# Up-projections of a ConvFFN: low parts of the input sums and of the first pair by adding transfers, and down's first pair prepared within the last pair of chunks

## The chip, the cores and the metric

The kernel runs on one core of a Trainium2 chip, in one launch. The metric is the device time of that launch in microseconds (us), and the time of a kernel is the median of several runs. The kernel before takes 1107.46 us (median of 3 runs, 1106.6 to 1108.25).

## The reference

The kernel computes a trunk of two layers over 512 tokens of 1024 features, in float32. Each layer is an attention mixer (a dilated window in the first, a forgetting attention in the second) and then a gated feed-forward network with a causal convolution of width 3 over the tokens. The change touches the feed-forward network (FFN) alone:

```python
def conv_ffn(xn, w_up, cw, cb, w_down):        # xn (1, 512, 1024), w_up (1024, 5632), w_down (2816, 1024)
    a = xn @ w_up
    T = a.shape[1]
    ap = jnp.pad(a, ((0, 0), (CONV_W - 1, 0), (0, 0)))
    a = sum(ap[:, j:j + T] * cw[j] for j in range(CONV_W)) + cb
    gate, val = jnp.split(a, 2, axis=-1)
    return (jax.nn.gelu(gate, approximate=True) * val) @ w_down
...
    h = h + rms_norm(mix, g[1])
    f = conv_ffn(rms_norm(h, g[2]), w_up[l], conv_w[l], conv_b[l], w_down[l])
    h = h + rms_norm(f, g[3])
```

## The kernel before

**High and low.** Each float32 product of two matrices is made of three matmuls on rounded operands (`mm3`, L294): high by high (L295), high by low (L296) and low by high (L297). So each operand, a weight or an activation, has to be split first: a high part, which is a rounded copy that the scalar engine (ACT) makes, and a low part, the operand less its high part. There are two ways to a low part. Either the vector engine (DVE) subtracts, once the high is there. Or ACT writes the negative of the rounded operand into the low's place ("minus"), and a transfer that GpSimd (POOL) issues adds the operand itself to it. The names are `added` in the pairs (L740 to 742), and `minus` and `low_added` for plain pieces.

**Weights.** A weight piece is 128x1024, 512 KB. The class `Weights` loads pieces by transfers from SyncE's queue, each as soon as a buffer is free, and splits them in the order of use: `high` (L58 the rounded copy, L69 the minus), `low` (L76, on DVE), `low_added` (L96). `ahead` says how many pieces `get` splits beyond the one that it hands out.

**The up-projection.** The 5632 columns are 22 chunks of 128 gate and 128 value columns. Chunks 0 to 3 are plain: one piece for the gate and one for the value, eight steps of `mm3` each. Chunks 4 to 19 are taken in eight pairs (`PAIRS`, two chunks each) by a scheme of seven products in place of eight: the four blocks of a pair's weights (A11, A21, A22 and A12: gate or value, first or second half of the features) are joined to S3 = A11 - A21, S1 = A21 + A22, S2 = S1 - A11 and S4 = A12 - S2, and tensor runs A11, S2, S3, A12, S1, A22 and S4, each of 24 matmuls on 128x256, in this order; A11 of the next pair comes between A22 and S4. The factors on the side of x are parts of x itself or sums of them, XA and XB, which `sums_in` makes once (L695 to L715) while chunks 0 to 3 run. Chunks 20 and 21 are plain again.

**The steps of a pair.** `prepare(p)` is a generator whose eight steps (up to a `yield` each) load, join and split a pair's weights, while tensor runs the pair before it: the high of A11; its low; S3's sum and high; the sum S1 (L756); the sum S2 (L758), its high, the high of A12; the lows of S2 (DVE) and A12 (GpSimd, L738), S1's high and adding transfer; the low of S3, the sum S4 (GpSimd, L770, which overwrites A12's raw tile in place), A22's high and adding transfer; and last S4's high and adding transfer. For the first pair the steps run while the plain chunks 2 and 3 run. In the loop over the pairs, `begin` runs product A11, `keep_first` copies it out of PSUM into `csum` (ACT, L1022), `sums` adds products together (DVE, L1044), and `ends` adds the last two (L1029, L1030). Product S2 writes the other half of the banks that `keep_first` reads, and product A12 adds into the first half again, while `sums` reads S2's half; each waits until those reads are done.

**Behind a chunk** stand the convolution's taps (ACT L670 or L657 scales and adds the bias, DVE L664 adds the two shifted taps), the gelu (ACT L689) and the product of gate and value (GpSimd L686), which a GpSimd transfer stores to DRAM (`hD`, L684).

**The down-projection** takes pairs of chunks by the same scheme: `pair_load` reads the activations back from `hD` (SyncE), `pair_sums` (DVE, L807 to L809) joins them, `pair_highs` (ACT, L817) and `pair_lows` (DVE, L821) split three operands of a pair. The first pairs are prepared while the last plain chunks run.

**The order.** Each engine runs its instructions in the order in which the code writes them; nothing is reordered. An instruction waits for its operands and for its buffers, and all that stands behind it on its engine waits with it. The buffers come from pools (16 tiles of 8 KB per partition, 10 of 4 KB, 8 of 2 KB, 8 PSUM banks), so a tile is free again when its last reader is done.

Of the kernel before, what the change touches and what calls it, by code (L numbers as in the profile page):

```python
# [115 lines left out]
def trunk_kernel(ctx, tc, x, norm_gains, w_qkv_a, w_o_a, w_q_b, w_o_b, kv_norm, w_kvf, b_f,  # L116
# [451 lines left out]
    def first_products(bd, n):  # L568
        bd.norm(3)
        outs = [bank([128, T], name="first") for _ in range(n)]  # L570
        ws = []
        for i, o in enumerate(outs):
            if i == 1:
                W.ahead -= 1
            ws.append(W.get())
            feat_mm(ws[i], bd.xT, o, LO)
            if i < 2:
                bd.transpose(2 + i)
            if i == 1:
                W.ahead += 1  # L580
        for w, o in zip(ws, outs):
            feat_mm(w, bd.xT, o, HI)
        return outs
# [65 lines left out]
    def ffn(l, bd, cp, nxt, ahead):  # L649
# [49 lines left out]
        def sums_in():  # L699
# [11 lines left out]
            for X, src in ((XA, v[0]), (XB, v[1])):  # L711
                X += [t8([128, 4, T], F32R, name="xsh"), t8([128, 4, T], F32R, name="xsl")]
                for k in (0, 2):
                    act.copy(X[0][:, k:k + 2], src[:, k:k + 2])
                    dve.tensor_tensor(X[1][:, k:k + 2], src[:, k:k + 2], X[0][:, k:k + 2].bitcast(F32), ALU.subtract)  # L715
                    yield
# [11 lines left out]
        def prepare(p):  # L728

# [13 lines left out]
            ga = grab(2)  # L745
            high("A11", ga)
            yield
            low("A11", ga)
            yield
            va = grab(1)  # L750
            s3 = t4([128, 1024], name="wsum")
            dve.tensor_tensor(s3, ga, va, ALU.subtract)
            high("S3", s3)
            yield
            vb = grab(1)
            dve.tensor_tensor(va, va, vb, ALU.add)  # L756
            yield
            dve.tensor_tensor(ga, va, ga, ALU.subtract)  # L758
            high("S2", ga)
            gb = grab(1)  # L760
            high("A12", gb)
            yield
            low("S2", ga)
            low("A12", gb, pool)
            high("S1", va)
            added("S1", va)
            W.load(W.n_split + 2)
            yield
            low("S3", s3)
            pool.tensor_tensor(gb, gb, ga, ALU.subtract)  # L770
            high("A22", vb)
# [7 lines left out]
        def prepare_last():  # L779

            W.load(W.n_split + 2)
            yield
            yield
            for added in (False, True, False, False):
                W.high(added)
                (W.low_added if added else W.low)()
                yield


# [188 lines left out]
        extra = sums_in()  # L978
        next(extra)
        post(0, first[0:2])  # L980
        next(extra)
        post(1, first[2:4])
        W.ahead = 1
        W.split(base + 7)
        W.high_added()
        steps = prepare(PAIRS[0])
        before = None
        for c in (2, 3):
            banks = [bank([128, T], name="up") for _ in range(2)]
            for s in range(2):  # L990
# [8 lines left out]
                for _ in range(3):  # L999
                    next(extra, None)  # L1000
                next(steps)
            before = c, banks
# [32 lines left out]
        for p in PAIRS:  # L1035
# [16 lines left out]
            bbs = [biased(*pend[0][:2])]  # L1052
            next(steps)
            times(p, "S3", o3, True)
# [33 lines left out]
        for _ in steps:  # L1088
            pass
        pair_sums(0)  # L1090
        banks = [begun[1], bank([128, T], name="up")]
# [4 lines left out]
        glu(pend[0][0], taps(*pend[0][:2]))  # L1096
        pair_highs(0)
        pair_sums(1)
        up(W.get(), banks[1], range(KD))
        post(*pend[1][:2])  # L1100
        before = NF - 2, banks
        banks = [bank([128, T], name="up") for _ in range(2)]
        up(W.get(), banks[0], range(KD))
        product()
        glu(before[0], taps(*before, lambda: pair_lows(0)))
        pair_highs(1)
        pair_sums(2)
        up(W.get(), banks[1], range(KD))
        before = NF - 1, banks
        post(*before, lambda: pair_lows(1))  # L1110
        pair_highs(2)
# [833 lines left out]
```

## Time and profile before

| | |
|---|---|
| median of 3 runs | 1107.46 us (1106.6 to 1108.25) |
| profiled execution, its time and its span | 1105.87 us, 1104.1 us |
| granted TensorE clock, mean | 0.993 |
| TensorE matmuls (PE), busy | 1083.4 us, 98% |
| TensorE weight loads (PEld) | 960.3 us, 87% |
| VectorE (DVE) | 900.8 us, 82% |
| ScalarE (ACT) | 683.8 us, 62% |
| GpSimd (POOL) | 306.8 us, 28% |
| transfers, mean | 220 GB/s |

The busy shares are means over a span in which stages with different limits follow one another: attention, feed-forward, attention, feed-forward. The places of FFN 1 that the prediction speaks of lie between 196 and 421 us; FFN 2 has the same ones some 583 us later. A row of the timeline gives the start in us, the length in us, the engine, the line, the operation, the tile written and those read, and in brackets how long the engine had been idle before it, and what ended that. A row of the windows gives the stretch, its length and then for each engine (matmul, weight load, DVE, ACT, POOL) the busy time and the count, then the granted clock, the transfers' share and the GB/s.

### The profile page before, as it was taken

How to read it: one execution, taken by the hardware profiler on the slowest of the kernel's cores; microseconds unless marked ns; L12 is line 12 of the kernel's file. 1: busy time of each engine (PE TensorE's matmuls, PEld its weight loads, DVE VectorE, ACT ScalarE, POOL GpSimd, SP SyncE). 2: the span in 40 equal slices, each digit the busy share in tenths (PEclk: the TensorE clock that was granted, in tenths of full speed). 3: DMA queues.
4: the chain of work that ended last, by engine and by line, in shares of the span. 5: the costliest groups of instructions: out<-in, count | busy, mean ns of one | idle time of the engine just before them, and what ended most of it. 6: DMA issues, size and time to landing. Idle time of an engine off the chain costs nothing.

```text
span 1104.1 us, 18905 instructions
## 1 busy us (share of the span) xinstructions
PE 1083.4 (98%) x6897; PEld 960.3 (87%) x6897; DVE 900.8 (82%) x1462; ACT 683.8 (62%) x1133; POOL 306.8 (28%) x318
## 2 busy tenths in 40 slices
PE   9999999979999999999999999999979999999997
PEld 7988889879999988888888888889879999987886
DVE  5898979868888799997686677868858888889995
ACT  6645765557676666576451577755467677656573
POOL 3543000264565532000001212100155566531000
PEclk9999999989999999999999999999989999999999
DMA  9799954378878978893447857774368878978962
GB/s 295 244 373 407 345 121 116 86 172 192 232 192 213 255 234 299 297 335 104 146 141 246 271 169 208 258 212 134 86 153 188 226 199 199 237 246 300 337 249 77
DMA packets 159509, 242.71 MB, mean 220 GB/s; under 512 B 12864, under 2 KB 106424, under 8 KB 159416
## 3 DMA queue, kind: packets, MB, share of 16 engines
q1 hardware_dynamic: 143784, 189.33, 52.2%
q0 software_dynamic: 14944, 52.18, 20.8%
q8 instruction: 54, 0.88, 0.3%
q14 instruction: 39, 0.32, 0.1%
q10 hardware_dynamic: 688, 0.01, 0.0%
HBM read 172.37 MB, written 39.73 MB: 192 GB/s over the span
## 4 chain that ended last, share of the span: by engine, by line
PE 88%; issue 5%; DVE 3%; ACT 2%; DMA 1%; POOL 1%; SPq 0%; DVEq 0%; POOLq 0%; ACTq 0%
PE up L295 9%; PE up L296 9%; PE up L297 9%; PE acc L297 9%; PE acc L295 8%; PE acc L296 8%; PE v_ps L295 2%; PE v_ps L296 2%; PE v_ps L297 2%; PE qk_ps L1396 2%; PE pT_ps L1786 2%; PE o_ps L1801 2%; PE s_ps L1752 2%; DVE w L821 1%; PE first L297 1%
## 5 line engine op out<-in xcount | busy, mean ns | idle before, releaser
L295 PE MATMUL up<-xsh,w 128*128 128x256 f32 x512 | 146.9, 287 | 12.5 <-ACT csum L1022 12.5
L296 PE MATMUL up<-xsl,w 128*128 128x256 f32 x512 | 146.4, 286 | 0.0
L297 PE MATMUL up<-xsh,w 128*128 128x256 f32 x512 | 146.3, 286 | 0.0
L734 ACT CAST w<-wraw 128x1024 fp32r<-128x1024 f32 x96 | 97.2, 1043 | 76.8 <-DVE wraw L758 59.1
L686 POOL TENSOR_TENSOR hc<-bb 128x512 f32<-128x512 f32 x44 | 76.7, 1743 | 226.6 <-ACT bb L689 143.2
L664 DVE SCALAR_TENSOR_TENSOR bb<-up,conv,bb 128x511 f32<-128x511 f32 (+1 forms) x160 | 118.7, 745 | 6.0 <-ACT bb L670 3.2
L297 PE MATMUL acc<-w 128*128 128x512 f32 (+1 forms) x311 | 120.6, 388 | 1.3 <-DVE w L821 1.3
L295 PE MATMUL acc<-w 128*128 128x512 f32 (+1 forms) x311 | 120.6, 388 | 0.0
L295 PEld LDWEIGHTS up<-xsh,w 128*128 128x128 f32 x512 | 100.0, 195 | 12.9 <-ACT csum L1022 12.9
L296 PE MATMUL acc<-w 128*128 128x512 f32 (+1 forms) x267 | 103.3, 387 | 0.0
L296 PEld LDWEIGHTS up<-xsl,w 128*128 128x128 f32 x512 | 100.0, 195 | 0.0
L297 PEld LDWEIGHTS up<-xsh,w 128*128 128x128 f32 x512 | 99.8, 195 | 0.0
L296 PE MATMUL up<-xbl,w 128*128 128x256 f32 (+1 forms) x256 | 79.3, 310 | 0.0
L296 PE MATMUL up<-xcl,w 128*128 128x256 f32 (+1 forms) x256 | 79.3, 310 | 0.0
L295 PE MATMUL up<-xbh,w 128*128 128x256 f32 (+1 forms) x256 | 79.3, 310 | 0.0
L295 PE MATMUL up<-xch,w 128*128 128x256 f32 (+1 forms) x256 | 79.2, 310 | 0.0
L297 PE MATMUL up<-xch,w 128*128 128x256 f32 (+1 forms) x256 | 79.2, 310 | 0.0
L297 PE MATMUL up<-xbh,w 128*128 128x256 f32 (+1 forms) x256 | 79.2, 309 | 0.0
L76 DVE TENSOR_TENSOR w<-wraw,w 128x1024 fp32r<-128x1024 f32 x54 | 64.5, 1218 | 16.1 <-ACT w L58 15.8
L58 ACT CAST w<-wraw 128x1024 fp32r<-128x1024 f32 x61 | 62.3, 1057 | 17.5 <-PE v_ps L296 6.9
L297 PEld LDWEIGHTS acc<-w 128*128 128x128 f32 x311 | 58.4, 188 | 14.0 <-DVE w L821 2.2
L295 PEld LDWEIGHTS acc<-w 128*128 128x128 f32 x311 | 58.4, 188 | 11.9
(309 smaller groups left out, 3153.6 us busy)
## 6 DMA issues: line engine op xcount, KB each, us to landing
wraw<-in_w_up_dram SPq DMA_DIRECT2D x88, 512.0 KB
w<-wraw POOLq DMA_DIRECT2D x56, 512.0 KB, 5.2
dT<-dsums SPq DMA_DIRECT2D x28, 512.0 KB
dsums<-in_w_down_dram SPq DMA_DIRECT2D x22, 512.0 KB
dsums<-in_w_down_dram SPq DMA_DIRECT2D x44, 256.0 KB
hD<-hc POOLq DMA_DIRECT2D x44, 256.0 KB, 6.2
dact<-hD SPq DMA_DIRECT2D x44, 256.0 KB
wraw<-dT SPq DMA_DIRECT2D x22, 512.0 KB
```

The lines of the kernel that those rows point to most:

```text
L58: (copy or self.nc.scalar.copy)(pair[:, 0], raw)
L76: self.nc.vector.tensor_tensor(pair[:, 1], raw, pair[:, 0].bitcast(F32), ALU.subtract)
L295: pe.matmul(o, ah, bh, start=first, stop=False, skip_group_check=shared)
L296: pe.matmul(o, ah, bl, start=False, stop=False, skip_group_check=shared)
L297: pe.matmul(o, al, bh, start=False, stop=last, skip_group_check=shared)
L664: dve.scalar_tensor_tensor(bb[:, s, n:], ps[:, :T - n], cp[:, 2 - n, ch:ch + 1], bb[:, s, n:], ALU.mult, ALU.add)
L686: pool.tensor_tensor(hc[c], bb[:, 0, :], bb[:, 1, :], ALU.mult)
L734: act.copy(w[a][:, 0], raw)
L1396: pe.matmul(qk_banks[b], a[n == 2], w[n == 1][:, kc % 2, :], start=kc + n == 0, stop=(kc, n) == (KD - 1, 2))
L1752: pe.matmul(sc[j, i][hh][:, :nn], qT[j][own, qp, i * 128:(i + 1) * 128], k[own, kp, :nn], start=qp + kp == 0, stop=qp == 1)
L1786: pe.transpose(o[:, k0 + k, :], p[:, hh, k * 128:(k + 1) * 128], ident)
L1801: pe.matmul(o[64 * hh:64 * hh + 64, i * 128:(i + 1) * 128], Vt[hd // 8][:, k, (hd % 8) * 64:(hd % 8) * 64 + 64], pT[j, i, hh][:, k, :], st ...
```

## The change

There are four parts, in both FFNs. The plain pieces 5 to 7 are split by minus and adding transfer, and `ahead` is set to 2 at the entry. The lows of XA and XB are made by a minus on ACT and an adding transfer in place of a subtraction on DVE. In the first pair of chunks alone, A11, S3 and A12 get their lows by adding transfers too, S2's sum goes to a tile of its own, and the last step (S4's high, minus and transfer) runs after product S2 has been written into the program, not with chunk 3. In the last pair, the four last plain pieces are split two steps earlier, and the steps so gained prepare the first pair of the down-projection; each later `pair_` call stands one place earlier.

```diff
@@ first_products
             if i == 1:
-                W.ahead += 1
+                W.ahead = 2
@@ sums_in
                 for k in (0, 2):
-                    act.copy(X[0][:, k:k + 2], src[:, k:k + 2])
-                    dve.tensor_tensor(X[1][:, k:k + 2], src[:, k:k + 2], X[0][:, k:k + 2].bitcast(F32), ALU.subtract)
+                    s = slice(k, k + 2)
+                    act.copy(X[0][:, s], src[:, s])
+                    act.activation(X[1][:, s], src[:, s], AF.Copy, scale=-1.0)
+                    pool.dma_start(X[1][:, s], src[:, s], accum_op=ALU.add)
                     yield
@@ prepare(p)
+            first = p == PAIRS[0]
...
             high("A11", ga)
+            if first:
+                added("A11", ga)
             yield
-            low("A11", ga)
+            if not first:
+                low("A11", ga)
...
             high("S3", s3)
+            if first:
+                added("S3", s3)
...
-            dve.tensor_tensor(ga, va, ga, ALU.subtract)
-            high("S2", ga)
+            s2 = t4([128, 1024], name="wsum") if first else ga
+            dve.tensor_tensor(s2, va, ga, ALU.subtract)
+            high("S2", s2)
             gb = grab(1)
             high("A12", gb)
+            if first:
+                added("A12", gb)
             yield
-            low("S2", ga)
-            low("A12", gb, pool)
+            low("S2", s2)
+            if not first:
+                low("A12", gb, pool)
...
-            low("S3", s3)
-            pool.tensor_tensor(gb, gb, ga, ALU.subtract)
+            if not first:
+                low("S3", s3)
+            pool.tensor_tensor(gb, gb, s2, ALU.subtract)
@@ prepare_last
-            W.load(W.n_split + 2)
-            yield
-            yield
             for added in (False, True, False, False):
...
+            pair_sums(0)
+            yield
+            pair_highs(0)
+            pair_sums(1)
+            yield
+            pair_lows(0)
+            yield
@@ ffn
         next(extra)
+        for _ in range(2):
+            W.high_added()
         post(0, first[0:2])
         next(extra)
+        W.high_added()
         post(1, first[2:4])
         W.ahead = 1
-        W.split(base + 7)
-        W.high_added()
...
-                next(steps)
+                if (c, s) != (3, 1):
+                    next(steps)
@@ the loop over the pairs
-            next(steps)
+            if p + 1 in PAIRS:
+                next(steps)
             times(p, "S3", o3, True)
@@ behind the pairs
-        pair_sums(0)
...
-        pair_highs(0)
-        pair_sums(1)
+        pair_highs(1)
         up(W.get(), banks[1], range(KD))
         post(*pend[1][:2])
+        pair_sums(2)
...
-        glu(before[0], taps(*before, lambda: pair_lows(0)))
-        pair_highs(1)
-        pair_sums(2)
+        glu(before[0], taps(*before, lambda: pair_lows(1)))
         up(W.get(), banks[1], range(KD))
         before = NF - 1, banks
-        post(*before, lambda: pair_lows(1))
+        post(*before)
```

The next rows are those of ACT in FFN 1 at the end of the first pair's preparation, before the change, from A12's high on (S2's high stands directly ahead of them in both kernels). `w_2314` is A12, `w_2319` S1, `w_2351` A22, `w_2357` S4 and `w_2418` A11 of the next pair; `bb` is a gelu and `csum` the copy of product A11.

```order
L734 CAST w_2314<-wraw_2270 128x1024
L689 ACTIVATE bb_2302<-bb_2302 128x512
L734 CAST w_2319<-wraw_2191 128x1024
L741 ACTIVATE w_2319<-wraw_2191 128x1024
L734 CAST w_2351<-wraw_2223 128x1024
L741 ACTIVATE w_2351<-wraw_2223 128x1024
L734 CAST w_2357<-wraw_2270 128x1024
L741 ACTIVATE w_2357<-wraw_2270 128x1024
L1022 COPY csum_2389<-up_2361 128x256
L1022 COPY csum_2389<-up_2363 128x256
L734 CAST w_2418<-wraw_2312 128x1024
```

The same place of ACT after the change, where the lines are 736 and 743 for 734 and 741, and 1040 for 1022; `w_2324` is A12, `w_2330` S1, `w_2361` A22, `w_2424` S4 and `w_2428` the next A11.

```order
L736 CAST w_2324<-wraw_2279 128x1024
L743 ACTIVATE w_2324<-wraw_2279 128x1024
L689 ACTIVATE bb_2311<-bb_2311 128x512
L736 CAST w_2330<-wraw_2183 128x1024
L743 ACTIVATE w_2330<-wraw_2183 128x1024
L736 CAST w_2361<-wraw_2225 128x1024
L743 ACTIVATE w_2361<-wraw_2225 128x1024
L1040 COPY csum_2395<-up_2367 128x256
L1040 COPY csum_2395<-up_2369 128x256
L736 CAST w_2424<-wraw_2279 128x1024
L743 ACTIVATE w_2424<-wraw_2279 128x1024
L736 CAST w_2428<-wraw_2322 128x1024
```

A12 has a minus more, S4's two operations stand behind the two copies instead of ahead of them, and the next A11 stands behind S4 as it did.

GpSimd's queue at the same place before the change. `hc` is the product of gate and value; `w_2193` is a plain piece, L738 the low of A12, L742 the adding transfers of S1, A22 and S4, L770 the sum S4.

```order
L686 TENSOR_TENSOR hc_2181<-bb_2171 128x512
L96 DMA w_2193<-wraw_2036 128x1024
L684 DMA hD_1936<-hc_2181 128x512
L686 TENSOR_TENSOR hc_2300<-bb_2183 128x512
L738 TENSOR_TENSOR w_2314<-wraw_2270,w_2314 128x1024
L742 DMA w_2319<-wraw_2191 128x1024
L770 TENSOR_TENSOR wraw_2270<-wraw_2270,wraw_2138 128x1024
L742 DMA w_2351<-wraw_2223 128x1024
L742 DMA w_2357<-wraw_2270 128x1024
L684 DMA hD_1936<-hc_2300 128x512
```

GpSimd's queue after the change, from A11 of the first pair (`w_2227`) on; `xsl` are the lows of XA and XB, `w_2267` is S3.

```order
L744 DMA w_2227<-wraw_2167 128x1024
L717 DMA xsl_2234<-xsum0_2157 128x1024 x2
L744 DMA w_2267<-wsum_2265 128x1024
L717 DMA xsl_2272<-xsum1_2158 128x1024 x2
L684 DMA hD_1936<-hc_2189 128x512
L686 TENSOR_TENSOR hc_2309<-bb_2191 128x512
L744 DMA w_2324<-wraw_2279 128x1024
L744 DMA w_2330<-wraw_2183 128x1024
L782 TENSOR_TENSOR wraw_2279<-wraw_2279,wsum_2318 128x1024
L744 DMA w_2361<-wraw_2225 128x1024
L744 DMA w_2424<-wraw_2279 128x1024
L684 DMA hD_1936<-hc_2309 128x512
```

Seven adding transfers stand ahead of S4's sum (L782) that GpSimd did not issue there before: A11, four for XA and XB, S3 and A12. The sum S4 overwrites `wraw_2279`, which A12's transfer reads.

VectorE at the end of the last pair in FFN 1, before the change: `dact_4095` is the first pair of the down-projection, L1029 and L1030 are the last two sums of the pair of chunks, `bb` the taps of its first chunk.

```order
L807 TENSOR_TENSOR dact_4095<-dact_4095 128x256
L808 TENSOR_TENSOR dact_4095<-dact_4095 128x256
L809 TENSOR_TENSOR dact_4095<-dact_4095 128x256
L1029 TENSOR_TENSOR up_4033<-up_4033,csum_4099 128x256
L1030 TENSOR_TENSOR up_4032<-up_4032,csum_4092 128x256
L1029 TENSOR_TENSOR up_4035<-up_4035,csum_4099 128x256
L1030 TENSOR_TENSOR up_4034<-up_4034,csum_4092 128x256
L664 SCALAR_TENSOR_TENSOR bb_4340<-up_4032,conv_1644,bb_4340 128x511
```

The same place after the change: `dact_4283` is the second pair of the down-projection, and `w_4311` to `w_4313` are the lows of the first.

```order
L823 TENSOR_TENSOR dact_4283<-dact_4283 128x256
L824 TENSOR_TENSOR dact_4283<-dact_4283 128x256
L825 TENSOR_TENSOR dact_4283<-dact_4283 128x256
L837 TENSOR_TENSOR w_4311<-wraw_4214,w_4311 128x1024
L837 TENSOR_TENSOR w_4312<-wraw_4250,w_4312 128x1024
L837 TENSOR_TENSOR w_4313<-dact_4105,w_4313 128x1024
L1047 TENSOR_TENSOR up_4043<-up_4043,csum_4109 128x256
L1048 TENSOR_TENSOR up_4042<-up_4042,csum_4102 128x256
L1047 TENSOR_TENSOR up_4045<-up_4045,csum_4109 128x256
L1048 TENSOR_TENSOR up_4044<-up_4044,csum_4102 128x256
L664 SCALAR_TENSOR_TENSOR bb_4371<-up_4042,conv_1644,bb_4371 128x511
```

The lows of the first down pair stand ahead of the closing sums, and the sums of its second pair stand where those of its first stood.

## The prediction

> **What bounds the kernel now.** I read the page's chain and its costliest groups first, then who the tensor engine waited for, then single instructions around those waits. From the page:
>
> ```profile
> PE 88%; issue 5%; DVE 3%; ACT 2%; DMA 1%; POOL 1%; SPq 0%; DVEq 0%; POOLq 0%; ACTq 0%
> L295 PE MATMUL up<-xsh,w 128*128 128x256 f32 x512 | 146.9, 287 | 12.5 <-ACT csum L1022 12.5
> ```
>
> The chain that ended last is tensor work for 88%, and one group holds the idle time. Tensor's waits (engine, line, releaser: total, times, longest):
>
> ```profile
> PE up L295 <- ACT csum L1022: 12.5, 2, 6.3
> PE acc L297 <- DVE w L821: 1.3, 2, 0.7
> ```
>
> So only tensor's waits are worth anything: one of 6.3 us in each FFN, and one of 0.7. The first, in FFN 1, in time (start, length, instruction, idle before); the last row is FFN 2's, 583.00 later:
>
> ```profile
> 220.68 0.28 PE L297 MATMUL up<-xbh,w 128*128 128x256 f32 x1
> 227.27 0.58 PE L295 MATMUL up<-xsh,w 128*128 128x256 f32 x1 [6.31 <-ACT csum L1022]
> 227.65 0.42 PE L296 MATMUL up<-xsl,w 128*128 128x256 f32 x1
> ...
> 230.64 0.36 PE L295 MATMUL up<-xsh,w 128*128 128x256 f32 x1
> 230.84 0.28 PE L296 MATMUL up<-xsl,w 128*128 128x256 f32 x1
> ...
> 234.67 0.28 PE L295 MATMUL up<-xbh,w 128*128 128x256 f32 x1
> 810.27 0.58 PE L295 MATMUL up<-xsh,w 128*128 128x256 f32 x1 [6.14 <-ACT csum L1022]
> 205.00:220.00 15.00, 15.00 (x76) 12.77 (x75) 11.74 (x13) 7.35 (x9) 0.99 (x1) 1.00 0.22 70
> 228.00:232.00 4.00, 4.00 (x25) 4.00 (x24) 3.19 (x3) 1.79 (x3) 2.84 (x4) 0.65 1.06 230
> ```
>
> At 227.27 product S2 of the first pair begins; A12, two products later, begins at 234.67. After the wait the matmuls stand 0.21 us apart until 230.64, afterwards 0.12; the two last rows, a table by stretch, give a granted clock of 1.00 before and 0.65 after. Those 3.37 us held 16 matmuls instead of 28: 12 x 0.12 = 1.46 us more. Without wait and slow clock A12 would begin at 220.68 + 0.12 + 48 x 0.12 = 226.6: **8.1 us are at stake per FFN**.
>
> Who was late is in the scalar engine's rows:
>
> ```profile
> 196.37 0.78 ACT L670 ACTIVATE bb<-first,conv 128x512 f32<-128x512 f32 x1 [3.35 <-PE first L297]
> 197.57 1.04 ACT L58 CAST w<-wraw 128x1024 fp32r<-128x1024 f32 x1
> 198.51 1.06 ACT L69 ACTIVATE w<-wraw 128x1024 fp32r<-128x1024 f32 x1
> ...
> 210.20 1.44 ACT L670 ACTIVATE bb<-up,conv 128x512 f32<-128x512 f32 x2
> 216.94 2.00 ACT L734 CAST w<-wraw 128x1024 fp32r<-128x1024 f32 x2 [5.29 <-DVE wraw L758]
> ...
> 224.96 1.04 ACT L734 CAST w<-wraw 128x1024 fp32r<-128x1024 f32 x1 [1.70 <-POOL wraw L770]
> 226.87 0.62 ACT L1022 COPY csum<-up 128x256 f32<-128x256 f32 x2
> 227.38 1.05 ACT L734 CAST w<-wraw 128x1024 fp32r<-128x1024 f32 x1
> ```
>
> The copy `csum` (226.87), which S2 waits for, stands behind S4's high and minus (224.96), and these behind GpSimd's sum for S4; S2's own high came at 216.94, released by DVE's sum.
>
> **The change, part by part.** All sums are for FFN 1; FFN 2 counts the same. VectorE and GpSimd in before:
>
> ```profile
> 212.80 2.97 DVE L664 SCALAR_TENSOR_TENSOR bb<-up,conv,bb 128x511 f32<-128x511 f32 x4
> 215.69 1.22 DVE L758 TENSOR_TENSOR wraw<-wraw 128x1024 f32<-128x1024 f32 x1
> 228.47 2.85 DVE L738 TENSOR_TENSOR w<-wraw,w 128x1024 fp32r<-128x1024 f32 x1 [5.88 <-ACT w L734]
> 231.24 0.41 DVE L1044 TENSOR_TENSOR csum<-up,csum 128x256 f32<-128x256 f32 x1
> 811.47 1.23 DVE L738 TENSOR_TENSOR w<-wraw,w 128x1024 fp32r<-128x1024 f32 x1 [5.88 <-ACT w L734]
> 221.66 0.89 POOL L742 DMA_DIRECT2D w<-wraw  x1 [0.16 <-issue]
> 222.28 2.64 POOL L770 TENSOR_TENSOR wraw<-wraw 128x1024 f32<-128x1024 f32 x1
> 228.62 1.61 POOL L686 TENSOR_TENSOR hc<-bb 128x512 f32<-128x512 f32 x1
> ```
>
> *Plain pieces 5 to 7.* Three lows leave VectorE; scalar gets two minus operations more ahead of the taps, inside its 3.35 us wait for tensor. They cost nothing: piece 5 is needed some 20 us after its adding transfer starts.
>
> *Sums of x, and the pair's first parts.* From 197.57 scalar runs A11, four of XA, S3, four of XB, each high now with its minus: 12 operations at the pitch of the rows (198.51 - 197.57 and its like, 0.955) end at 209.0. The taps follow there instead of at 210.20. VectorE has shed the lows that stood ahead of them, so its taps start with scalar's first (209.0 + 0.78 = 209.8, not 212.80), take 2.97, and its sum for S2 1.22: 213.9 in place of 216.91. Scalar goes on with nine operations to the copy (S2; A12 and minus; the gelu at half length; S1 and minus; A22 and minus): 8 x 0.955 less what the half saves, 221.15. Copy to S2 took 0.40 before (226.87 to 227.27), so **S2 begins at 221.55**: a wait of 0.6 us in place of 6.3, as S4's pair of operations now stands behind the copy.
>
> *What is late next: A12.* It waits for VectorE's first sum into `csum` (231.24 in before, 3.0 us before it was needed). In VectorE's queue that sum stands behind the low of the next pair's A11, which waits for its high on scalar, which stands behind S4's high and minus, which wait for GpSimd's sum for S4. And this sum overwrites A12's input in place, so it now waits until A12's adding transfer has landed; before, it waited for a GpSimd low. From that landing: sum to S4's high 224.96 - 222.28 = 2.68; high and minus 226.87 - 224.96 = 1.91; A11's high to VectorE 228.47 - 227.38 = 1.09; low 1.23 (row 811.47); sum 0.41: **7.3 us**. Queued behind it on VectorE are the next pair's sums, for which scalar waits.
>
> The transfer: A12's minus ends at 216.95, its issue 0.3 later, 217.3. Time to landing of these adds (least, median, most), and one add alone in 40 slices of 221 to 226:
>
> ```profile
> DMA to landing us min/median/max: 4.5/5.2/7.9
> DMA  0000000000000000091990959909739199095010
> ```
>
> The one issued at 221.66 moves from 223.1 to 225.9: 2.6 to 2.8 us. The change issues six (A11, XA twice, S3, XB twice) 1.9 us apart from 199.9, faster than one is moved; in a row from 201.35 they end at 217, and with two weight loads and a store among them up to 221. So A12's landing is bounded by 217.3 + 4.6 = 221.9 and 217.3 + 7.9 = 225.2. I take 6.2, the middle, since it has a queue ahead: 223.5. **A12 begins at 223.5 + 7.3 = 230.8, 3.87 us before 234.67** (bounds 229.2 and 232.5: 5.5 and 2.2). S2 and S3 end at 221.55 + 48 x 0.12 = 227.3, so tensor waits 3.5 us there.
>
> *Later pairs.* Does the lead last? The same two rows of VectorE a pair apart, and its sums in the second pair:
>
> ```profile
> 238.15 1.21 DVE L758 TENSOR_TENSOR wraw<-wraw 128x1024 f32<-128x1024 f32 x1
> 242.07 0.43 DVE L1044 TENSOR_TENSOR up<-up,csum 128x256 f32<-128x256 f32 x1 [2.71 <-PE up L297]
> 251.48 0.41 DVE L1044 TENSOR_TENSOR csum<-up,csum 128x256 f32<-128x256 f32 x1
> 258.30 1.22 DVE L758 TENSOR_TENSOR wraw<-wraw 128x1024 f32<-128x1024 f32 x1
> ```
>
> The ring VectorE, scalar, GpSimd, scalar, VectorE turns in 258.30 - 238.15 = 20.15; tensor needs 7 x 24 x 0.12 = 20.16. In the second pair tensor comes to A12 at 230.8 + 20.16 = 251.0, the sum at about 251.48 less the 0.4 to 1.6 by which the ring is earlier: level. I count nothing off, and up to 0.5.
>
> *Down's first pair, and the last pieces two steps earlier.* The 0.67 us (413.13) is spent on the lows of down's pair 1, done at 413.07; these move ahead of the last chunk's taps and are in time. Next late are the lows of pair 2:
>
> ```profile
> 408.34 3.59 DVE L821 TENSOR_TENSOR w<-wraw,w 128x1024 fp32r<-128x1024 f32 x2
> 411.86 1.21 DVE L821 TENSOR_TENSOR w<-dact,w 128x1024 fp32r<-128x1024 f32 x1
> 413.13 0.50 PE L297 MATMUL acc<-w 128*128 128x512 f32 x1 [0.67 <-DVE w L821]
> 415.68 3.90 DVE L821 TENSOR_TENSOR w<-wraw,w 128x1024 fp32r<-128x1024 f32 x2
> 419.50 1.21 DVE L821 TENSOR_TENSOR w<-dact,w 128x1024 fp32r<-128x1024 f32 x1
> ```
>
> They end at 420.71. Without the wait tensor wants them 36 matmuls of 0.23 after 412.46, at 420.75. VectorE's work up to there is the same but for one low less (1.2 earlier), while the closing sums of the last pair now stand behind pair 0's lows and their scalar highs; a collision with GpSimd's product as at 228.47 costs up to 1.6. Bounds: 0.67 gained, 0.9 lost; I take **0**.
>
> **Sum:** 2 x 3.87 = 7.7 us. The profiled execution (1105.87; its span is 1104.1) would become 1098.2; the median shown, 1107.46, is 1.6 above it, so the forecast is **1099.7**.
>
> **Rivals.** *The clock falls in the new wait.* If 3.5 us suffice where 6.3 did (and 0.67 did not, since the matmul after 413.13 keeps its pitch), 1.46 comes back per FFN: 2 x 2.4 = 4.8 gained, 1102.6. The Trainium skill (TensorE: Matmul & The Clock Gate, "HAM oscillation — how this bites in real kernels") warns of idle gaps above about 3.4 us; its own text has that window run free, so that a gap just above need not hold a whole one. Here the slow stretch of 3.37 us agrees with the figure; the threshold itself no row shows.
>
> *VectorE shut out.* Row 228.47 took 2.85 us beside GpSimd's product at 228.62, its twin 811.47 only 1.23. If the low of A11 meets that product in both FFNs, A12 is 1.6 later: 2 x 2.25 = 4.5, 1103.0. Speaking against: the low now follows S4's minus sooner, some 0.5 us ahead of the product. The Trainium skill (SBUF — State Buffer, "SBUF: two separate sides") says that whichever starts first holds the shared ports for its whole instruction; by it the low wins, yet row 228.47, which by its start was first, lost.
>
> *Both*, a wait of 5 us with the clock falling: 2 x 0.8, 1105.9, no change that can be told.
>
> *All goes well*: a landing after 4.6 us, both down waits gone: 2 x 5.5 + 1.3 = 12.3, 1095.2.
>
> *Slower: the adding queue.* A12 stands where it stood if its transfer lands at 234.67 - 7.3 = 227.4, ten us after issue; beyond that each us costs one per FFN. At 4 us per add beside the loads (between 2.7 alone and the 6.4 that a landing of 7.9 leaves) six end at 225.4, a store at 226.4, A12 at 230.4: A12 begins 3.0 late, 2 x 3.0, 1113.5. For it: the adds come faster than one is moved, and A22's tile also waits for XB's. Against: none of the adds landed later than 7.9.
>
> **How the numbers follow.** Forecast 0.42; all well 0.13; clock 0.14; shut out 0.09; both 0.11; adding queue 0.11. Beyond 0.2% (2.2 us, about what a measurement of this kernel can tell from none): faster 0.42 + 0.13 + 0.14 + 0.09 = 0.78; same 0.11; slower 0.11. The range, 1094.5 to 1106.5, takes in all but the queue case and tails.
>
> **What would show it.** Right: the wait of L295 for `csum` falls from 6.3 to about 0.6 us (up to 2 if XB's adds hold up A22's high), and a new wait of 2 to 4 us stands before the first A12, released by VectorE's `csum` sum; GpSimd's sum for S4 sits idle until an add lands. The clock rival shows as a granted clock of 0.65 after that wait; the queue rival as landings above 8 us; the down step as a wait before L297 `acc` that is gone or has moved to pair 2. Wrong would be: no wait at A12, which makes it 1095 or less, or waits in every later pair, by which the lead is given back.

## The result

The changed kernel takes 1112.13 us (median of 5 runs, 1109.46 to 1115.5), beside 1107.46 us (1105.76 to 1108.25) for the kernel before: 1.0051 times the time, interval 1.0026 to 1.0076. Forecast were 1099.7 us and faster; it is slower by about 5 us, outside the range. The profiled execution of the change took 1109.46 us (span 1107.7), 3.6 us more than that of before; it is the shortest of the five.

From the page of the changed kernel, the chain; and the rows of tensor's waits (engine, tile, line, releaser: total, times, longest):

```profile
PE 87%; DMA 4%; issue 3%; POOL 2%; DVE 2%; ACT 1%; SPq 0%; DVEq 0%; ACTq 0%; POOLq 0%
PE up L295 <- DVE csum L1062: 11.3, 2, 6.0
PE acc L297 <- DVE w L837: 3.3, 2, 1.7
PE up L295 <- ACT csum L1040: 1.0, 2, 0.5
```

The wait before S2 went from 12.5 to 1.0 us in all, as forecast. In its place stand two waits, 11.3 us in all, for VectorE's `csum` ahead of A12, and transfers, which had 1% of the chain before, now have 4%. The wait in down grew from 1.3 to 3.3 us. In time, with two rows of the windows (the first number after the counts of GpSimd is the granted clock):

```profile
222.00 0.39 PE L295 MATMUL up<-xsh,w 128*128 128x256 f32 x1 [0.50 <-ACT csum L1040]
...
227.74 0.28 PE L297 MATMUL up<-xsh,w 128*128 128x256 f32 x1
233.33 0.58 PE L295 MATMUL up<-xbh,w 128*128 128x256 f32 x1 [5.31 <-DVE csum L1062]
...
236.89 0.29 PE L296 MATMUL up<-xbl,w 128*128 128x256 f32 x1
...
817.89 0.58 PE L295 MATMUL up<-xch,w 128*128 128x256 f32 x1 [5.97 <-DVE csum L1062]
233.00:237.00 4.00, 3.67 (x17) 3.67 (x18) 3.96 (x7) 1.38 (x3) 1.67 (x2) 0.52 1.06 210
818.00:822.00 4.00, 4.00 (x19) 4.00 (x20) 3.96 (x7) 1.68 (x2) 1.23 (x2) 0.50 1.04 212
```

S2 begins at 222.00, 5.3 us earlier than before; A12 at 233.33, only 1.3 us earlier. Behind that wait the clock is 0.5, and the matmuls stand 0.21 us apart instead of 0.12.

Who was late at A12, in the rows of the scalar engine, VectorE and GpSimd, and the landing of the transfer issued at 217.69 (last column of the last row):

```profile
221.61 0.61 ACT L1040 COPY csum<-up 128x256 f32<-128x256 f32 x2
228.75 1.04 ACT L736 CAST w<-wraw 128x1024 fp32r<-128x1024 f32 x1 [6.53 <-POOL wraw L782]
...
231.72 1.22 DVE L740 TENSOR_TENSOR w<-wraw,w 128x1024 fp32r<-128x1024 f32 x1 [14.98 <-ACT w L736]
232.86 0.75 DVE L1062 TENSOR_TENSOR csum<-up,csum 128x256 f32<-128x256 f32 x2
...
217.69 0.88 POOL L744 DMA_DIRECT2D w<-wraw  x1 [5.05 <-ACT w L743]
...
226.34 2.37 POOL L782 TENSOR_TENSOR wraw<-wraw,wsum 128x1024 f32<-128x1024 f32 x1 [5.38 <-DMA w<-wraw]
w<-wraw POOLq DMA_DIRECT2D x1, 512.0 KB, 8.5
```

It is the chain that the prediction named: A12's transfer, S4's sum on GpSimd, S4's high, the next A11's high, its low, the sum. From the start of GpSimd's sum, which stands 0.1 us behind the landing, it takes 233.33 - 226.34 = 7.0 us (7.3 forecast). But the transfer landed 8.5 us after its issue, at 226.2, not at 223.5. What moved from 220 to 222.5 (queue: packets, MB, share of the 16 engines):

```profile
q1 hardware_dynamic: 775, 0.77, 92.4%
q0 software_dynamic: 21, 0.07, 14.8%
```

q1 carries the weight loads, q0 GpSimd's transfers. A12's transfer was issued behind six others, the last of which landed at 219.3, and a store, landed at 220.6; then two weight loads took nearly all 16 engines for some 2.5 us. No run separates the queue from the loads.

Set side by side by the start of the same matmul in both timelines, the change stands behind before by:

| place | FFN 1 | FFN 2 |
|---|---|---|
| ahead of the FFN | 0.54 | 1.26 |
| S2's first matmul | -5.27 | -4.37 |
| A12's first matmul | -1.34 | -0.08 |
| later pairs, once the clock is back | 0.29 | 2.66 |
| down, behind its second and third pair | 1.30 | 3.54 |

So the up part moved -0.25 us in FFN 1 and +1.40 in FFN 2, the down part +1.01 and +0.88. The rest is the 0.54 us from ahead of FFN 1, which the change doesn't touch.

Down's loss stands in these rows (the scalar engine's, VectorE's and tensor's):

```profile
398.09 1.99 ACT L833 CAST w<-wraw 128x1024 fp32r<-128x1024 f32 x2
399.98 1.05 ACT L833 CAST w<-dact 128x1024 fp32r<-128x1024 f32 x1
400.93 1.44 ACT L670 ACTIVATE bb<-up,conv 128x512 f32<-128x512 f32 x2
...
401.73 2.97 DVE L664 SCALAR_TENSOR_TENSOR bb<-up,conv,bb 128x511 f32<-128x511 f32 x4 [2.83 <-ACT bb L670]
...
421.36 1.21 DVE L837 TENSOR_TENSOR w<-dact,w 128x1024 fp32r<-128x1024 f32 x1
...
422.62 0.50 PE L297 MATMUL acc<-w 128*128 128x512 f32 x1 [1.72 <-DVE w L837]
```

The scalar engine makes the highs of down's pair 1 ahead of the taps (L670) that VectorE waits for; VectorE sits idle for 2.83 us, and the lows of pair 2 are done at 422.57 instead of 420.71. (In before VectorE had one such idle time there too, of 1.58 us.)

### The profile page after: what moved, and what is told of

It reads as the page before. It is cut to its first block, busy times and chain, and to the rows that moved or that the text cites. A ratio compares the mean times of both kernels' runs of the same rounds, so it can differ in the third digit from the quotient of the medians.

```text
span 1107.7 us, 18966 instructions
## 1 busy us (share of the span) xinstructions
PE 1084.8 (98%) x6897; PEld 961.5 (87%) x6897; DVE 886.9 (80%) x1446; ACT 699.7 (63%) x1151; POOL 316.4 (29%) x334
## 4 chain that ended last, share of the span: by engine, by line
PE 87%; DMA 4%; issue 3%; POOL 2%; DVE 2%; ACT 1%; SPq 0%; DVEq 0%; ACTq 0%; POOLq 0%
PE up L295 11%; PE up L297 11%; PE up L296 11%; PE acc L297 8%; PE acc L295 8%; PE acc L296 8%; PE v_ps L295 2%; PE v_ps L296 2%; PE v_ps L297 2%; PE pT_ps L1802 2%; PE o_ps L1817 2%; DMA w<-wraw 2%; PE s_ps L1768 2%; PE first L297 1%; PE qk_ps L295 1%
## 5 line engine op out<-in xcount | busy, mean ns | idle before, releaser
L295 PEld LDWEIGHTS up<-xsh,w 128*128 128x128 f32 x512 | 98.7, 193 | 1.4 <-ACT csum L1040 1.4
L297 PEld LDWEIGHTS up<-xsh,w 128*128 128x128 f32 x512 | 98.6, 192 | 0.0
L295 PE MATMUL up<-xch,w 128*128 128x256 f32 (+1 forms) x256 | 80.6, 315 | 6.0 <-DVE csum L1062 6.0
L297 PE MATMUL up<-xch,w 128*128 128x256 f32 (+1 forms) x256 | 80.4, 314 | 0.0
L740 DVE TENSOR_TENSOR w<-wraw,w 128x1024 fp32r<-128x1024 f32 x28 | 46.8, 1671 | 37.7 <-ACT w L736 37.7
L76 DVE TENSOR_TENSOR w<-wraw,w 128x1024 fp32r<-128x1024 f32 x50 | 60.2, 1222 | 18.4 <-ACT w L58 14.2
L297 PEld LDWEIGHTS acc<-w 128*128 128x128 f32 x311 | 58.4, 188 | 16.0 <-DVE w L837 4.2
```

What stands on the lines that cost most here:

```text
L76: self.nc.vector.tensor_tensor(pair[:, 1], raw, pair[:, 0].bitcast(F32), ALU.subtract)
L295: pe.matmul(o, ah, bh, start=first, stop=False, skip_group_check=shared)
L297: pe.matmul(o, al, bh, start=False, stop=last, skip_group_check=shared)
L740: engine.tensor_tensor(w[a][:, 1], raw, w[a][:, 0].bitcast(F32), ALU.subtract)
```

## The experiments

Each kernel was timed against the kernel before, on the same chip. They are numbered in the order in which they stand here, from the first to the eleventh. The theory from the traces was: the late landing of A12's transfer and the slow clock behind its wait took back what S2 won, and down cost 1 us per FFN. The rivals: the loss lies in one of the two parts alone, or the chain behind the landing is the cause and not the landing.

### The two parts apart

The change with the down part left as before (`prepare_last`, the loop's second step and all `pair_` calls):

```diff
-            if p + 1 in PAIRS:
-                next(steps)
+            next(steps)
...
-        pair_highs(1)
+        pair_highs(0)
+        pair_sums(1)
```

> The change without its down part: the last pieces, and the first pairs of the down-projection, are prepared where they were before. Theory: in the two profiles the up part alone moves tensor by -0.2 us in FFN 1 and +1.2 us in FFN 2 (the start of S2 won 5.3 us, a late A12 with a second slow clock gave it back), the down part by +0.9 and +1.0. So this kernel stands about 1 us over before (up to 3, as the landing of A12's adding transfer falls), 1108.5 to 1110.5, with a wait of 5 to 6 us at A12 and the old one of 0.7 at down's pair 1. Rival, the loss is all in the down part and the up part pays as forecast: 1100.

Measured: 1107.56 us, 1.0007 times before (0.9999 to 1.0016). The waits at A12 are there (11.3 us in all), those in down are the old 1.3. The up part gains nothing and loses next to nothing, less than the 1 us expected. The opposite, before with the down part alone:

> The kernel before with the down part of the change alone. Theory: the wait of 0.7 us at down's pair 1 goes and one of 1.6 to 1.7 at pair 2 comes, since VectorE sits 2.8 us behind the highs of pair 1 on the scalar engine: +1.8 us over before. Rival, the late lows of pair 2 come from the later up-projection and not from the order: no wait at pair 2, and 1.3 us faster.

Measured: 1108.56 us, 1.0015 times before (1.0006 to 1.0024), with waits of 1.6 us at pair 2 in down in both FFNs; the 0.9 us in the median are half of what was expected. So the order, and not a later up-projection, makes VectorE late there. The parts add up to 0.2%, the change has 0.5%; the difference is taken up below.

### The wait at A12 taken away, in two ways

The change with the next A11's high ahead of S4's step in the first pair:

```diff
+            if p == PAIRS[0]:
+                next(nxt_steps)
             for _ in steps:
                 pass
             steps = nxt_steps
-            next(steps)
+            if p != PAIRS[0]:
+                next(steps)
```

> The change, with the high of the next pair's A11 written ahead of S4's step in the first pair, so that VectorE's sum into csum no longer stands behind S4. Theory, that this chain and not A12's own low holds A12: the sum is done by about 225.3, A12 waits only for its own transfer (226.3) and starts when S3 ends, 227.9, without a wait or a slow clock: 5.4 + 1.6 us per FFN, 14 to 16 us under the change, 1096 to 1098. Rival 1, A12's own adding transfer is what it waits for: the wait of 5 us stays, and the time with it. Rival 2, S4 becomes late, since its transfer lands at about 237 to 239 and is needed at 239.4: a wait before S4 of up to 4 us, 8 us worse than the theory.

And the change with the first pair's A12 low on GpSimd again:

```diff
             high("A12", gb)
-            if first:
-                added("A12", gb)
             yield
             low("S2", s2)
-            if not first:
-                low("A12", gb, pool)
+            low("A12", gb, pool)
```

> The change, with the first pair's A12 low made by GpSimd as before, not by an adding transfer. Theory, that the late landing of A12's transfer (8.5 us after issue) set everything behind it: GpSimd's low at about 216.4 to 218.9, S4's sum at about 220.7 to 223.1, S4's high and minus by 225.1, next A11's high 226.2, low 227.4, sum 227.8: A12 begins at about 228 with next to no wait and full clock, 13 to 15 us under the change, 1097 to 1099; a wait of up to 2 us may come in the second pair. Rival, the queue of adding transfers is late by itself, and the ones of S1 and A22 hold S1 or A22 instead: waits of 2 to 5 us there, and 1104 to 1108.

Both did at A12 what the theory said, and neither became faster: 1114.19 us (1.0064, 1.005 to 1.0078) and 1112.24 us (1.0046, 1.0034 to 1.0058). Tensor's waits in the first of them:

```profile
PE up L295 <- DVE csum L1062: 8.7, 14, 0.8
PE acc L297 <- DVE w L837: 6.1, 4, 2.0
PE up L295 <- ACT csum L1040: 2.0, 3, 1.0
PE up L297 <- DMA w<-wraw: 2.0, 2, 1.7
```

The two waits at the first A12 are gone, and fourteen have come, one in each later pair of both FFNs, of 0.3 to 0.8 us. In FFN 1 the kernel with GpSimd's low wins 7.8 us on before in the first pair (it is 1.58 behind ahead of the FFN and 6.18 ahead after that pair), and after the last pair it is 0.13 ahead: 6 of them are gone. The theory that the late A12 alone kept the gain away fell here: **the lead itself is given back**, at up to 1 us per pair. Rival 2 of the third kernel, a wait for S4's transfer, did not show. The waits for a transfer, 0.3 us in FFN 1 and 1.7 in FFN 2, are for A22's, which stands behind S4's sum in GpSimd's queue.

Where the microsecond comes from: a whole turn of a pair in the third kernel (VectorE's low of A11, its low of S2, GpSimd's low of A12 and sum S4, the scalar engine's highs, the next low of A11):

```profile
311.94 1.23 DVE L740 TENSOR_TENSOR w<-wraw,w 128x1024 fp32r<-128x1024 f32 x1 [3.94 <-ACT w L736]
...
323.23 1.21 DVE L740 TENSOR_TENSOR w<-wraw,w 128x1024 fp32r<-128x1024 f32 x1
...
323.37 3.35 POOL L740 TENSOR_TENSOR w<-wraw,w 128x1024 fp32r<-128x1024 f32 x1 [1.01 <-ACT w L736]
...
327.28 2.79 POOL L782 TENSOR_TENSOR wraw<-wraw 128x1024 f32<-128x1024 f32 x1
...
330.10 1.05 ACT L736 CAST w<-wraw 128x1024 fp32r<-128x1024 f32 x1 [1.96 <-POOL wraw L782]
...
333.07 1.22 DVE L740 TENSOR_TENSOR w<-wraw,w 128x1024 fp32r<-128x1024 f32 x1 [3.94 <-ACT w L736]
```

The ring turns in 333.07 - 311.94 = 21.13 us; tensor needs 20.16. In before, VectorE's sum ahead of its low of S2, that low, and GpSimd's low of A12:

```profile
324.15 0.43 DVE L1044 TENSOR_TENSOR up<-up,csum 128x256 f32<-128x256 f32 x1 [1.01 <-PE up L297]
324.50 1.40 DVE L738 TENSOR_TENSOR w<-wraw,w 128x1024 fp32r<-128x1024 f32 x1
...
322.40 2.41 POOL L738 TENSOR_TENSOR w<-wraw,w 128x1024 fp32r<-128x1024 f32 x1 [1.00 <-ACT w L734]
```

In before VectorE has to wait for tensor ahead of its low of S2, which so starts when GpSimd's low of A12 is nearly done. When tensor leads, VectorE's low starts 0.14 us ahead of GpSimd's, and GpSimd's takes 3.35 us instead of 2.41: 0.94 of the 0.97 us that the ring is too long. The same two lows in the change itself:

```profile
324.79 2.28 DVE L740 TENSOR_TENSOR w<-wraw,w 128x1024 fp32r<-128x1024 f32 x1
...
323.57 2.41 POOL L740 TENSOR_TENSOR w<-wraw,w 128x1024 fp32r<-128x1024 f32 x1 [1.00 <-ACT w L736]
```

There tensor is late again by the wait at A12 and the slow clock, so GpSimd's low starts first: it keeps its 2.41 us and VectorE's takes 2.28 instead of 1.22. VectorE has that time to spare, the ring turns in 20.2 us, and the later pairs of the change give nothing back.

### Two kernels that did not test the ring

To take A12's low out of the ring, S4's sum got a tile of its own, ahead of that low; in the second kernel the low was made by an adding transfer in all pairs, and the highs of down's pair 1 moved (below).

```diff
             low("S2", s2)
+            s4 = t4([128, 1024], name="wsum")
+            pool.tensor_tensor(s4, gb, s2, ALU.subtract)
             low("A12", gb, pool)
...
-            pool.tensor_tensor(gb, gb, s2, ALU.subtract)
...
-            high("S4", gb)
-            added("S4", gb)
+            high("S4", s4)
+            added("S4", s4)
```

> The fourth kernel (A12's low in the first pair by GpSimd), with the sum S4 in a tile of its own, written ahead of A12's low on GpSimd in every pair. Theory: where tensor has a lead, the ring VectorE, scalar, GpSimd, scalar, VectorE turns in 21.14 us a pair instead of 20.16, because GpSimd's low of A12 then falls beside VectorE's low of S2 (3.35 us instead of 2.41) and stands ahead of S4's sum. With S4's sum first the low leaves the ring: the 0.3 to 0.7 us at A12 in each later pair go (8.6 us in all), and the lead of about 5 us per FFN stays; the waits in down stay, 1.5 and 2.0 with slow clocks behind them: 1103 to 1105. Rival: the two engines hinder each other whatever stands first, so S4's sum is the slow one instead, the waits stay, 1111 to 1113.

> The change, with A12's low by an adding transfer in all pairs, S4's sum in a tile of its own in all pairs, and the highs of down's pair 1 on the scalar engine behind the taps of the last paired chunk, not ahead of them. Theory: GpSimd makes only S4's sum and the product in a pair, the ring gets 3 to 5 us shorter than tensor's 20.16, there is no wait at A12 in any pair and no slow clock, and down's two waits go: 6 to 7 us per FFN under the kernel before, 1093 to 1097. Rival: with four adding transfers a pair they land 8 us after issue as in the first pair, and hold A12 or S1 in every pair: 1105 to 1112.

Measured: 1118.37 us (1.009, 1.0074 to 1.0106) and 1122.41 us (1.0132, 1.0115 to 1.0149). The waits at A12 in the later pairs are gone in both, but others came. The scalar engine's wait in the first kernel, in the pairs from 260 to 380 us, and one of its rows in the second:

```profile
ACT bb L657 <- DMA w<-wraw: 17.0, 6, 3.6
```

```profile
390.07 1.04 ACT L58 CAST w<-wraw 128x1024 fp32r<-128x1024 f32 x1 [10.26 <-DMA wraw<-in_w_up_dram]
```

The tile of S4 comes from the pool that the taps' tiles come from, and is held until an adding transfer has landed: the taps wait 3 us a pair for a buffer. In the second the scalar engine waited 10.26 us for a weight load; most likely the raw tiles, which are held longer there too, made that load late. Neither expectation held, and with these new waits neither kernel tells anything on the ring.

### Down's highs

The change with one line moved:

```diff
         glu(pend[0][0], taps(*pend[0][:2]))
-        pair_highs(1)
         up(W.get(), banks[1], range(KD))
         post(*pend[1][:2])
+        pair_highs(1)
         pair_sums(2)
```

> The change, with the highs of down's pair 1 on the scalar engine behind the taps of the last paired chunk. Theory: VectorE's 2.8 us behind those highs go, so the lows of pair 2 are in time, the waits of 1.7 and 1.6 us in down go, and with them the slow clocks that follow them in some executions and spread the change's times over 6 us: 1106 to 1108, within 2 us of each other. Rival: what the change costs beyond its two parts run alone does not come from these waits: 1110 to 1112 and as wide a spread.

Measured: 1106.12 us, 0.9994 times before (0.9984 to 1.0003); eleven runs, ten of them from 1105.18 to 1108.12 and one of 1111.03. The expectation held: this one line is worth 6 us of the change's time. VectorE runs eight taps in a row, and the waits in down are 0.2 us in all:

```profile
397.61 5.94 DVE L664 SCALAR_TENSOR_TENSOR bb<-up,conv,bb 128x511 f32<-128x511 f32 x8 [0.25 <-ACT bb L670]
PE acc L297 <- DVE w L837: 0.2, 1, 0.2
```

The change itself was run again, for a second profile:

> The change unaltered, for a second profile of it beside the same chip's runs. Theory: 1109 to 1115 again, and where this execution is longer than the first profile's 1109.5, the excess stands as a later landing of A12's adding transfer or as a granted clock of about 0.5 behind one of the waits (A12, down's pair 2), 1.5 to 2.5 us each. Rival: the excess lies outside the FFNs.

Measured: 1112.62 us (1.0045, 1.0032 to 1.0058), 1110.13 to 1114.35; the profiled execution is again the shortest.

```profile
PE acc L297 <- DVE w L837: 3.9, 2, 2.0
```

Its waits in down are 1.9 and 2.0 us. The excess that the expectation looked for is not in this profile, since it is the shortest run. But the third and fourth kernels have such waits with the clock falling behind them. Here is the third's in FFN 1; the granted clock is 0.52 from 426.5 to 429.5 us:

```profile
425.35 0.50 PE L297 MATMUL acc<-w 128*128 128x512 f32 x1 [1.98 <-DVE w L837]
425.69 0.39 PE L295 MATMUL acc<-w 128*128 128x512 f32 x1
...
427.46 0.63 PE L295 MATMUL acc<-w 128*128 128x512 f32 x1
427.89 0.63 PE L296 MATMUL acc<-w 128*128 128x512 f32 x1
428.32 0.63 PE L297 MATMUL acc<-w 128*128 128x512 f32 x1
```

The matmuls go from 0.23 to 0.43 us apart for some eight of them, which costs 1.6 us, from 1.3 us after a wait of 1.98 on. This profiled run, 1116.47 us, is one of the longest of the third kernel: it holds two such falls, and its mean clock is 0.996, where the shortest run, 1111.65 us, has 0.998. That the longer runs of the change hold one or two of them too is likely, and would make up the 2.5 us between its profiled run and its median. Its second set of runs fits: the mean clock is 0.995 in the shortest and 0.992 in the four others. In the first set three of the four longer runs fit (0.994 against 0.991 to 0.992), and one of 1115.08 us, with 0.995, does not. No profile of a longer run of the change was taken, so this stays open.

The same order cost only 0.9 us in the second experiment; its two waits, of 1.6 us, are shorter than any in down behind which the clock fell in these traces (1.78 us at the least, in the fourth kernel).

### The ring

The fourth kernel with the highs moved, as a base; then the same without VectorE's low of S2 in the later pairs. The product S2 uses its high in the low's place there, so this kernel leaves out the low part of S2's factor. Last the change with A12's low on VectorE in all pairs, and the highs moved; it leaves nothing out.

The first diff shows the split alone, not the product's own edit.

```diff
-            low("S2", s2)
+            if first:
+                low("S2", s2)
```

```diff
-            low("S2", s2)
-            if not first:
-                low("A12", gb, pool)
+            for a, raw in (("S2", s2), ("A12", gb))[::1 if first else -1]:
+                low(a, raw)
```

> The fourth kernel (A12's low in the first pair by GpSimd) with the highs of down's pair 1 behind the taps, as in the seventh: the kernel beside which the next one is read. Theory: no wait at the first A12, waits of 0.3 to 0.7 us at A12 in each later pair (about 8.6 us in all), and down's waits gone or small; the fourth kernel's 1112.2 less the 6 us that this step was worth in the seventh: 1106. Rival, the up part is worth a gain as soon as down is mended: 1100 or less.

> The ninth kernel without VectorE's low of S2 in the pairs behind the first: the product S2 takes its high in the low's place there, with the same matmuls, so that its results lack that part. Theory, that GpSimd's low of A12 takes 3.35 instead of 2.41 us because VectorE's low of S2 runs beside it, and that this sets the ring at 21.14 us a pair: the low takes 2.4, the ring turns in 20.2, the later waits at A12 go but for 0.1 each, and the time falls 6 to 8 us under the ninth, 1098 to 1100. Rival, GpSimd's low is slow beside whatever VectorE runs (its taps take that place): 3 us or more, waits of 0.3 to 0.7 still there, 1104 to 1106.

> The change, with A12's low made by VectorE in all pairs (ahead of S2's low but in the first pair), and the highs of down's pair 1 behind the taps. Theory: the first A12 waits for no landing; in the later pairs A12's low takes 1.2 us instead of 2.4 to 3.4 on GpSimd, and nothing of VectorE's stands beside S4's sum, so the ring turns in about 18.5 us, less than tensor's 20.16; VectorE has 3.9 us idle a pair and pays 1.2 of it. No waits at A12, the lead of 6 to 7 us per FFN kept, down's waits gone: 1092 to 1096. Rival, VectorE becomes the bound (17.9 of 20 us a pair busy before this, up to 1.6 more where it meets GpSimd): waits of 0.5 us and more in each pair, 1102 to 1108.

| | time, us | times before | interval |
|---|---|---|---|
| A12's low on GpSimd, highs moved | 1105.39 | 0.9982 | 0.9973 to 0.9991 |
| ... without VectorE's low of S2 | 1094.21 | 0.9879 | 0.9865 to 0.9892 |
| A12's low on VectorE, highs moved | 1089.57 | 0.9837 | 0.9824 to 0.985 |

GpSimd's low of A12 in the seven later pairs of FFN 1 (total, mean ns), in before, in the fourth kernel, and without VectorE's low of S2:

```profile
L738 POOL TENSOR_TENSOR w<-wraw,w 128x1024 fp32r<-128x1024 f32 x7 | 16.9, 2412 | 7.0 <-ACT w L734 7.0
```

```profile
L740 POOL TENSOR_TENSOR w<-wraw,w 128x1024 fp32r<-128x1024 f32 x7 | 23.4, 3339 | 7.0 <-ACT w L736 7.0
```

```profile
L740 POOL TENSOR_TENSOR w<-wraw,w 128x1024 fp32r<-128x1024 f32 x7 | 17.7, 2531 | 7.0 <-ACT w L736 7.0
PE up L295 <- DVE csum L1063: 0.5, 2, 0.3
```

The ninth kernel did what its expectation said at A12; in down it still waits 2.6 us. Without VectorE's low beside it GpSimd's low is back at 2.5 us, the fourteen waits of 8.6 us are two of 0.5 in all, and the time falls by 11 us. That is more than the 6 to 8 expected, which counted the waits alone: in the ninth kernel's traces a wait of 0.73 us puts tensor back by 0.98. VectorE also has 1.2 us less to do in a pair here, but it was not short of time: in the ninth kernel it waits 3.93 us for the scalar engine ahead of the next low of A11. That settles it: this meeting of the two engines makes the ring longer than tensor's work. Most of the lead is kept from the first pair to the last (7.8 us and 7.3 left in FFN 1, 7.9 and 6.2 in FFN 2). The Trainium skill (SBUF — State Buffer, "Who interferes with whom") says that a VectorE instruction with two inputs in SBUF contends with a GpSimd instruction that reads SBUF; the rows agree, GpSimd's low being 0.81 us shorter on average without VectorE's.

With A12's low on VectorE there is nothing of tensor's waits left in either FFN. The rows of VectorE's low of A11 there, a pair apart:

```profile
305.00 1.23 DVE L740 TENSOR_TENSOR w<-wraw,w 128x1024 fp32r<-128x1024 f32 x1 [0.58 <-ACT w L736]
...
324.94 1.23 DVE L740 TENSOR_TENSOR w<-wraw,w 128x1024 fp32r<-128x1024 f32 x1 [0.58 <-ACT w L736]
```

The ring turns in 19.94 us (18.5 expected), under tensor's 20.16, and VectorE waits 0.58 us for the scalar engine where it waited 3.94. This kernel beats both others: 16 to 18 us under before, 7.8 us in each FFN from the first pair, and 0.9 to 1.0 from down. The expectation said 1092 to 1096.

## Why the prediction was wrong, step by step

In the profiled run the forecast of 7.7 us gained became 3.6 us lost, by these steps. Up to A12's first matmul 1.9 us are gained in FFN 1 (-1.34 less 0.54) and 1.3 in FFN 2 (-0.08 less 1.26), not 3.87 each. The slow clock behind it costs 1.6 and 2.7, down costs 1.0 and 0.9, and 0.5 stand ahead of FFN 1.

**What bounds the kernel, and S2: right.** The wait of 6.3 us fell to 0.5 (0.6 forecast); S2 began at 222.00 (221.55 forecast, and the change was 0.54 us behind ahead of the FFN).

**A12's landing: the mechanism right, the size wrong, beyond its bounds.** The named chain held A12, and 7.3 us was 7.0. The landing was put at 223.5, at most 225.2, from landings of 4.5 to 7.9 us in before. Here the transfer stood behind a queue and then met two loads, and landed 8.5 us after issue, at 226.2. The slower rival named such a queue with loads, and its sign, landings above 8 us, came true; its point was ten us after issue, and the truth lies between the two. That its time of 1113.5 is near the measured 1112.13 is luck: it had A12 begin 3.0 us late in each FFN, and nothing lost to the clock or in down.

**The clock: the rival came true.** The forecast held the wait of 3.5 us too short; it became 5.3 and 6.0, and the clock fell. By the table, tensor loses 1.63 us behind A12 in FFN 1 (-1.34 to 0.29) and 2.74 in FFN 2 (-0.08 to 2.66), where before runs at full clock; before paid its 1.46 ahead of A12. The two losses differ as the slow stretches do, some 3.5 us at a clock of 0.5 in FFN 1 and some 6 in FFN 2. The rival of a wait of 5 us with the clock falling (1105.9) was the nearest for the up part alone, 1107.6.

**"I count nothing off" for the later pairs: true of the change as it ran, wrong for the lead that the sum counted on.** In the change tensor's distance to before stays the same from the second pair to the last, 0.29 us in FFN 1 and 2.66 in FFN 2. But it had no lead left to lose. The sum took a lead of 3.87 us as kept, since ring and tensor both turned in 20.15. That was the ring while tensor is late: then VectorE waits for tensor, and its low of S2 does not start ahead of GpSimd's low. With a lead the ring turns in 21.13, as in the third and fourth kernels; in the fourth's FFN 1 the later pairs eat 6 of 7.8 us. So a landing on time would not have brought the forecast either. A lead of just 3.87 us was not run; that it would have gone the same way is argued from those two kernels. The last sentence of the prediction named waits in every later pair as a sign of being wrong, and gave them no price.

**Down: put at 0, cost 0.9 to 1.4 us per FFN in the profiles and 6 us in the median.** The term counted VectorE's work up to pair 2's lows and found it equal but for one low; the failing step is that it did not count VectorE's idle time. The scalar highs that it named were pair 0's. Those of pair 1 (2.8 us) stand ahead of the taps that VectorE waits for. With them behind the taps, in the seventh kernel, down loses 3.0 to 3.7 us less than in the two profiles of the change, about half of the 6; the other half is most likely the clock behind those waits, which no profile of the change shows.

**VectorE shut out by GpSimd's product at A12: did not occur.** The low of A11 at 231.72 took 1.22 us. The collision between the two engines that decided, in the kernels with a lead, was another, in the later pairs.

## What to carry to other kernels

A single long wait at the front of a pipeline can hide a ring of other engines that is a little too slow once the bound engine is ahead. Before a wait is valued, sum that ring's operations as they would run with the bound engine ahead, with each meeting of two engines whose operations slow each other; if the sum is over the bound engine's period, removing the wait only spreads it, and the ring has to be shortened first. And where a step is moved on one engine, look at what the engine behind it will sit idle for, not only at the sum of its work.

## What was not expected of the hardware

- VectorE's and GpSimd's subtractions of 128x1024 float32 beside each other: GpSimd's takes 3.34 us instead of 2.41 when VectorE's begins 0.14 us ahead of it (fourth kernel). When GpSimd's begins 1.2 us ahead (the change), it takes 2.41, and VectorE's 2.28 instead of 1.22.
- The clock fell behind waits of 1.96 and 1.98 us (third kernel) and 1.78 and 2.02 us (fourth) in down, and not behind waits there of 1.72 us (the change), 1.90 and 2.00 us (its second profile) or 1.98 us (fifth kernel), so the length of the wait alone does not decide it. The Trainium skill (TensorE: Matmul & The Clock Gate, "HAM oscillation — how this bites in real kernels") speaks of gaps above about 3.4 us; these rows differ from that.
- Six adding transfers of 512 KB issued 1.9 us apart (the change) landed after 5.0, 5.6, 6.4, 7.3, 8.1 and 9.4 us: the landings stand 2.5 to 3.2 us apart, so the later ones waited for the earlier.
